# State-space core of a two-layer backbone: where clips, sums and one broadcast are computed

## The chip, the cores and the metric

The kernel runs on one core of a Trainium2 chip. The metric is the device time of one execution in microseconds (us). The kernel before took 1882.75 us in the median of three runs (1881.45 to 1883.67). Its engines are TensorE (PE, matrix products), VectorE (DVE), ScalarE (ACT, table functions and scaled copies), GpSimd (POOL) and SyncE (SP, which issues most transfers). Matrix products read SBUF and write to PSUM banks, which the other engines empty.

## The reference

Two layers work on 256 latent and 256 context tokens of width 1024. Each layer makes one modulated norm and one input projection, feeds three token mixers (a bidirectional state-space scan, a windowed attention, a latent attention), merges them by gates and ends with an FFN. All is fp32. In the last layer the context tokens only feed the mixers and have no output of their own. Cut to what the change touches:

```python
silu_c, silu_cc = silu(c), silu(c_ctx)              # rows of the modulation
mod = silu_c @ w_mod[i] + b_mod[i]                  # and the same with silu_cc
# state-space branch, 16 heads of 64 in 2 groups, chunks of 128 tokens, state of 128
acs  = cumsum(dt * a)                               # per head, along the chunk
y_diag[i] = sum_j (C_i . B_j) exp(acs_i - acs_j) dt_j x_j      # j <= i, in the chunk
state     = sum_j exp(acs_end - acs_j) dt_j B_j x_j            # leaves the chunk
h_next    = h * exp(acs_end) + state
y_off[i]  = exp(acs_i) (C_i . h)
y = y_forward + reverse(y_backward) + d_skip * x    # both directions
out = rms_norm(y * silu(z), norm_g)
```

The context's last state is the latent tokens' first, in each direction.

## The kernel before, in words

Tokens are four tiles of 128: latent 0 and 1, context 2 and 3. In fp32 a large product is made of three products of rounded parts (`hi` and `lo` of the weights by L132 on ScalarE and L134 on VectorE; the products are L146, L147 and L148). Weights come in blocks `raw`; four `raw`, three `hi` and three `lo` blocks turn round. PSUM has four banks named `mm`, two `s` and two `t`.

`ssm_core` works on steps (group, tile, half of four heads): 16 in layer 0, where all four tiles have an output, 8 in layer 1, where only two have. For each step a matrix of decay exponents per head and direction is fetched by a transfer that spreads one row over 128 partitions (`ef` and `eb`, two tiles of 128x512, L873). Then the step runs through five stages, each one step behind the one before:

- `first`: clip both against the token's own sum, per head (four 128x128 pieces: `ef` by ScalarE at L889, `eb` by VectorE at L890), combine them on GpSimd (L891), and scale the product of C and B (`cb`) by dt (L895).
- `second`: the exponential (L901), dt for the other direction (L905), and the product of both (L906).
- `third`: four small products into one `s` bank (L917); after the second half GpSimd multiplies x by d_skip (L920), the states' products go through `t` banks (L925, scaled by L927 into `yo`), and L929 adds the `s` bank to x.
- `fourth`: GpSimd adds both `yo` (L935). `fifth`: the gate with z and its square sum (L941, L943).

Beside the steps run the state chains: `state_x` multiplies x by its weight on GpSimd (L848, `xd`), `state` makes one product into an `s` bank (L856) and either copies it (L140 on VectorE or L142 on ScalarE, `hst`) or adds it to the decayed state before (L861 and L862). There are six chains per group, two per step in both layers: one for each of the four context passes, and one for each of the two latent tiles that hand on to the other.

`weave` lays the core among the work that fills it (z projection, keys and values, gates): it takes parts of the fill by a cost per step (`F_SSM`). The order on each engine is that of the program; an engine does not overtake itself. So an instruction waits also for all that stands in front of it on its engine.

The rows of silu(c) and silu(c_ctx) are loaded as 2x512 pieces in `masks` (L193 to L200), and `mod_rows` spreads each over 128 partitions by a product with a selecting matrix (L245) and a ScalarE copy (L247). `mod_dve` reduces the modulation weights against them on VectorE (L260).

Of the kernel before, what the change touches and what calls it, by code (L numbers as in the profile page):

```python
# [19 lines left out]
P = 128  # L20
# [67 lines left out]
class Kern:  # L88
# [102 lines left out]
    def masks(self):  # L191
        nc, c = self.nc, self.c
        self.crowd = [self.U(name="crow") for _ in range(2)]  # L193
        for j in range(2):
            nc.sync.dma_start(self.crowd[j][0:2, :], self.d["crow"][:, j * 512 : j * 512 + 512])
        for t in self.crowd:
            th = self.U(name="cth")
            nc.scalar.activation(th[0:2, :], t[0:2, :], AF.Tanh, scale=0.5)
            nc.vector.scalar_tensor_tensor(t[0:2, :], th[0:2, :], 1.0, t[0:2, :], ALU.add, ALU.mult)
            nc.vector.tensor_scalar(t[0:2, :], t[0:2, :], 0.5, None, ALU.mult)  # L200
        self.identb = c.tile([P, P], BF16, name="identb")
        nc.vector.tensor_copy(self.identb, self.ident)
        self.maskb = c.tile([P, 2, P], BF16, name="maskb")
        nc.gpsimd.tensor_scalar(self.maskb[:, 0, :], self.tril, -NEG, NEG, ALU.mult, ALU.add)
        nc.gpsimd.tensor_scalar(self.maskb[:, 1, :], self.triu, -NEG, NEG, ALU.mult, ALU.add)
# [30 lines left out]
    def mod_rows(self):  # L236
        nc = self.nc
        self.nmod = 0
        sel = self.c.tile([P, 2, P], F32, name="sel")
        self.crow = []  # L240
        for s in range(2):
            nc.vector.tensor_copy(sel[0:2, s, :], self.ident[0:2, s : s + 1].to_broadcast([2, P]))
            for j in range(2):
                ps = self.PS("s")
                nc.tensor.matmul(ps, sel[0:2, s, :], self.crowd[j][0:2, :], start=True, stop=True)  # L245
                t = self.U(name="crow")
                nc.scalar.activation(t, ps, AF.Copy)  # L247
                self.crow.append(t)

    def mod_dve(self, l, ch):  # L250
        nc = self.nc
        for m in range(8):
# [3 lines left out]
            for s in range(2):  # L256
                o = self.mod[l][:, ch * 8 + m, s : s + 1]
                for j in range(2):
                    junk = self.S([P, 512], "junk", dt=BF16, bufs=1)
                    nc.vector.tensor_tensor_reduce(junk, raw[j], self.crow[2 * s + j], 1.0,  # L260
# [569 lines left out]
    def ssm_core(self, l, tts, fill):  # L830
# [10 lines left out]
        chains = [(g, *c) for g in range(2) for c in ((2, 0, None, 3), (3, 1, None, 2), (3, 0, 3, 0), (2, 1, 2, 1), (0, 0, 0, 1), (1, 1, 1, 0))]  # L841
        hin, xds = {}, {}

        def state_x(i):
            if i < len(chains):
                g, tt, dr, _, _ = chains[i]
                xd = xds[i] = self.U(name="xd")
                nc.gpsimd.tensor_tensor(v8(xd), v8(self.xs[tt, g]), b64(self.wd[:, tt, dr, hs(g)]), ALU.mult)  # L848

        def state(i):  # L850
            if i >= len(chains):
                return
            g, tt, dr, prev, to = chains[i]
            bt = self.btok[tt // 2][:, (tt % 2) * 256 + g * P : (tt % 2) * 256 + g * P + P]
            ps = self.PS("s")
            nc.tensor.matmul(ps, bt, xds.pop(i), start=True, stop=True)  # L856
# [3 lines left out]
            else:  # L860
                nc.vector.tensor_tensor(v8(hn), v8(hin[g, dr, prev]), b64(self.etot[:, tt, dr, hs(g)]), ALU.mult)  # L861
# [15 lines left out]
        def first(i):  # L877
# [8 lines left out]
            for j in range(4):  # L886
                hh = 8 * g + 4 * q + j
                sl = [e[dr][:, j * P : (j + 1) * P] for dr in range(2)]
                nc.scalar.activation(sl[0], sl[0], AF.Relu, scale=-1.0, bias=self.fg[:, tt, 0, hh : hh + 1])  # L889
                nc.vector.tensor_scalar(sl[1], sl[1], self.fg[:, tt, 1, hh : hh + 1], 0.0, ALU.subtract, ALU.min)  # L890
            nc.gpsimd.tensor_tensor(e[0], e[1], e[0], ALU.subtract)  # L891
# [6 lines left out]
        def second(i):  # L898
            g, tt, q = steps[i]
            e, cb = eb[i], tile_[g, tt]  # L900
            nc.scalar.activation(e[0], e[0], AF.Exp)  # L901
# [6 lines left out]
        def third(i):  # L908
# [9 lines left out]
            if q == 1:  # L918
# [10 lines left out]
                nc.vector.tensor_tensor(xs, xs, yds.pop((g, tt)), ALU.add)  # L929
# [17 lines left out]
        si = 0  # L947
        n = len(steps)
        for i in range(2):
            loads(i)  # L950
            state_x(i)
        for i in range(n + 4):
# [3 lines left out]
            state(si)  # L956
            state(si + 1)
            state_x(si + 2)
            state_x(si + 3)
            si += 2  # L960
# [399 lines left out]
    def layer(self, l, x, h, norm):  # L1360
# [19 lines left out]
        drain(fill)  # L1380
        q = [self.swa_q(l, h, g, tts) for g in range(2)]
# [14 lines left out]
        if not last:  # L1396
            self.mod_rows()
# [271 lines left out]
```

## Time and profile before

| | us | share of the span |
|---|---|---|
| profiled execution, its own time | 1882.14 | |
| its span | 1880.0 | |
| TensorE busy | 1812.1 | 96% |
| VectorE busy | 1436.7 | 76% |
| ScalarE busy | 889.5 | 47% |
| GpSimd busy | 351.0 | 19% |

The span begins with the first instruction and ends with the last; some 2 us of the execution lie around it. Times in the rows below are counted from its start. The core of layer 0 lies at about 150 to 310 us, that of layer 1 at about 1287 to 1390 us. Busy shares are means over the program; within the cores TensorE is less busy and VectorE more than over the whole.

### The profile page before, as it was taken

How to read it: one execution, taken by the hardware profiler on the slowest of the kernel's cores; microseconds unless marked ns; L12 is line 12 of the kernel's file. 1: busy time of each engine (PE TensorE's matmuls, PEld its weight loads, DVE VectorE, ACT ScalarE, POOL GpSimd, SP SyncE). 2: the span in 40 equal slices, each digit the busy share in tenths (PEclk: the TensorE clock that was granted, in tenths of full speed). 3: DMA queues.
4: the chain of work that ended last, by engine and by line, in shares of the span. 5: the costliest groups of instructions: out<-in, count | busy, mean ns of one | idle time of the engine just before them, and what ended most of it. 6: DMA issues, size and time to landing. Idle time of an engine off the chain costs nothing. (4 is left out here: it accounts for less than half of the span.)

```text
span 1880.0 us, 28523 instructions
## 1 busy us (share of the span) xinstructions
PE 1812.1 (96%) x10188; PEld 1541.4 (82%) x10188; DVE 1436.7 (76%) x3162; ACT 889.5 (47%) x1931; POOL 351.0 (19%) x297
## 2 busy tenths in 40 slices
PE   8998999999999999999999999998889999999999
PEld 2786777788878888898888888886779988899999
DVE  3888886798799885569988875898878677777654
ACT  3555564444555653343222222546545676555442
POOL 3004434200012331100000000012433245410000
PEclk9999999999999999999999999999899999999999
DMA  8334252355343233535555553435233332255564
GB/s 296 96 107 138 92 177 88 123 194 171 134 153 114 97 118 117 186 117 191 189 203 191 182 160 105 126 100 179 95 128 117 122 105 73 86 182 172 187 177 138
DMA packets 102181, 269.18 MB, mean 143 GB/s; under 512 B 12836, under 2 KB 15700, under 8 KB 102040
## 3 DMA queue, kind: packets, MB, share of 16 engines
q1 hardware_dynamic: 93320, 253.02, 41.3%
q10 hardware_dynamic: 7056, 9.85, 1.5%
q0 software_dynamic: 1664, 4.50, 0.6%
q8 instruction: 80, 1.31, 0.3%
q14 instruction: 61, 0.50, 0.1%
HBM read 255.66 MB, written 11.67 MB: 142 GB/s over the span
## 5 line engine op out<-in xcount | busy, mean ns | idle before, releaser
L132 ACT ACTIVATE hi<-raw 128x1024 fp32r<-128x1024 f32 (+1 forms) x350 | 356.7, 1021 | 586.6 <-PE mm L147 301.8
L134 DVE TENSOR_TENSOR lo<-raw,hi 128x1024 fp32r<-128x1024 f32 (+3 forms) x346 | 420.5, 1217 | 202.9 <-ACT hi L132 201.2
L146 PE MATMUL mm<-hh,hi 128*128 128x512 f32 (+1 forms) x1280 | 439.0, 345 | 3.5 <-ACT sq L683 1.9
L148 PE MATMUL mm<-hh,lo 128*128 128x512 f32 (+1 forms) x1280 | 436.4, 342 | 0.9 <-DVE lo L134 0.9
L147 PE MATMUL mm<-hl,hi 128*128 128x512 f32 (+1 forms) x1280 | 436.6, 342 | 0.6 <-DVE hl L353 0.5
L146 PEld LDWEIGHTS mm<-hh,hi 128*128 128x128 f32 x1280 | 242.1, 190 | 32.3 <-ACT sq L683 2.2
L148 PEld LDWEIGHTS mm<-hh,lo 128*128 128x128 f32 x1280 | 242.8, 190 | 28.7 <-DVE lo L134 1.3
L147 PEld LDWEIGHTS mm<-hl,hi 128*128 128x128 f32 x1280 | 243.0, 190 | 28.3 <-DVE hl L353 1.2
L146 PE MATMUL mm<-hi,hh 128*128 128x512 f32 (+2 forms) x368 | 146.2, 398 | 4.5 <-DVE z L826 2.5
L147 PE MATMUL mm<-lo,hh 128*128 128x512 f32 (+2 forms) x368 | 141.2, 384 | 0.3 <-DVE lo L134 0.3
L148 PE MATMUL mm<-hi,hl 128*128 128x512 f32 (+2 forms) x368 | 137.7, 383 | 2.0 <-DVE hl L353 2.0
L260 DVE CUSTOM_DVE_ANT_0 junk<-mraw,crow,mod 128x512 bf16<-128x512 f32 x160 | 120.3, 752 | 4.8 <-DMA mraw<-in_w_modT 2.3
L260 DVE CUSTOM_DVE_ANT_0 junk<-mraw,crow 128x512 bf16<-128x512 f32 x160 | 110.3, 690 | 9.5 <-DMA mraw<-in_w_modT 7.9
L638 ACT ACTIVATE prob<-s,nm 128x512 f32<-128x512 f32 (+1 forms) x96 | 59.2, 617 | 65.5 <-DVE nm L635 35.1
L146 PEld LDWEIGHTS mm<-hi,hh 128*128 128x128 f32 x368 | 70.7, 192 | 20.1 <-DVE z L826 5.0
L160 POOL TENSOR_TENSOR nrs<-nv,mhalf 128x2 f32<-128x2 f32 x7 | 5.2, 748 | 436.1 <-DVE nv L301 436.1
L153 ACT ACTIVATE pth<-t 128x256 fp32r<-128x256 f32 x160 | 60.7, 387 | 52.0 <-DVE ptl L154 43.3
L147 PEld LDWEIGHTS mm<-lo,hh 128*128 128x128 f32 x368 | 70.6, 192 | 14.1 <-issue 4.1
L148 PEld LDWEIGHTS mm<-hi,hl 128*128 128x128 f32 x368 | 69.6, 191 | 14.8 <-DVE hl L353 2.5
L146 PE MATMUL mm<-acth,hi 128*128 128x512 f32 (+1 forms) x198 | 72.7, 367 | 0.6 <-DVE xl L1346 0.6
L147 PE MATMUL mm<-actl,hi 128*128 128x512 f32 (+1 forms) x198 | 72.3, 365 | 0.0
L148 PE MATMUL mm<-acth,lo 128*128 128x512 f32 (+1 forms) x198 | 72.3, 365 | 0.0
(434 smaller groups left out, 4125.6 us busy)
## 6 DMA issues: line engine op xcount, KB each, us to landing
raw<-in_w_fi SPq DMA_DIRECT2D x88, 512.0 KB, 3.3
mraw<-in_w_modT SPq DMA_DIRECT2D x160, 256.0 KB, 4.6
raw<-in_w_g SPq DMA_DIRECT2D x48, 512.0 KB, 3.3
raw<-in_w_p SPq DMA_DIRECT2D x48, 512.0 KB, 3.3
raw<-in_w_fo SPq DMA_DIRECT2D x32, 512.0 KB, 3.9
raw<-in_w_xbc SPq DMA_DIRECT2D x24, 512.0 KB, 3.5
wm<-in_w_mod SPq DMA_DIRECT2D x32, 256.0 KB, 5.6
raw<-in_w_z SPq DMA_DIRECT2D x16, 512.0 KB, 3.2
```

The source lines that it names most:

```text
L132: nc.scalar.activation(hi[:, :n], raw[:, :n], AF.Copy)
L134: eng.tensor_tensor(lo[:, :n], raw[:, :n], hi[:, :n].bitcast(F32), ALU.subtract)
L146: mm(out, a[0], b[0], start=start, stop=False)
L147: mm(out, a[0], b[1], start=False, stop=False)
L148: mm(out, a[1], b[0], start=False, stop=stop)
L153: nc.scalar.activation(hi, src, AF.Copy)
L160: self.nc.gpsimd.tensor_tensor(out, v, self.mhalf[:, 0 : v.free_size()], ALU.pow)
L260: nc.vector.tensor_tensor_reduce(junk, raw[j], self.crow[2 * s + j], 1.0, o if j else 0.0, ALU.mult, ALU.add, o)
L638: nc.scalar.activation(pt[:, :nk], ps[:, :nk], AF.Exp, bias=nm, scale=scale, accum_out=den)
```

## The change

Four edits, all in or near the core.

1. The rows of silu(c) come by four transfers that spread a row of 512 over 128 partitions, issued behind the fill of the core; tanh and its product are then made on 128x512. The factor one half moves into the reduction. The products and copies of L245 and L247 are gone.
2. In layer 1 the two context tiles make one state sum per direction: the weights `wd` of the farther tile are first multiplied by the nearer one's decay, and two products add up in one bank. Chains per group go from six to four, and a plan says which chains belong to which step.
3. Both clips are ScalarE's (`Relu` with scale -1 gives the negative of what VectorE gave), so GpSimd adds, and the exponential takes the scale -1.
4. The inner product's bank is added to the first `yo` instead of x.

```diff
-        self.crowd = [self.U(name="crow") for _ in range(2)]
-        for j in range(2):
-            nc.sync.dma_start(self.crowd[j][0:2, :], self.d["crow"][:, j * 512 : j * 512 + 512])
-        for t in self.crowd:
-            th = self.U(name="cth")
-            nc.scalar.activation(th[0:2, :], t[0:2, :], AF.Tanh, scale=0.5)
-            nc.vector.scalar_tensor_tensor(t[0:2, :], th[0:2, :], 1.0, t[0:2, :], ALU.add, ALU.mult)
-            nc.vector.tensor_scalar(t[0:2, :], t[0:2, :], 0.5, None, ALU.mult)
...
         self.crow = []
         for s in range(2):
-            nc.vector.tensor_copy(sel[0:2, s, :], self.ident[0:2, s : s + 1].to_broadcast([2, P]))
             for j in range(2):
-                ps = self.PS("s")
-                nc.tensor.matmul(ps, sel[0:2, s, :], self.crowd[j][0:2, :], start=True, stop=True)
                 t = self.U(name="crow")
-                nc.scalar.activation(t, ps, AF.Copy)
+                nc.sync.dma_start(t.rearrange("p (a w) -> p a w", a=1), self.d["crow"][s : s + 1, j * 512 : j * 512 + 512].partition_broadcast(P))
                 self.crow.append(t)
+        yield
+        for t in self.crow:
+            th = self.U(name="crth")
+            nc.scalar.activation(th, t, AF.Tanh, scale=0.5)
+            nc.vector.scalar_tensor_tensor(t, th, 1.0, t, ALU.add, ALU.mult)
...
-                    nc.vector.tensor_tensor_reduce(junk, raw[j], self.crow[2 * s + j], 1.0,
+                    nc.vector.tensor_tensor_reduce(junk, raw[j], self.crow[2 * s + j], 0.5,
...
-        chains = [(g, *c) for g in range(2) for c in ((2, 0, None, 3), (3, 1, None, 2), (3, 0, 3, 0), (2, 1, 2, 1), (0, 0, 0, 1), (1, 1, 1, 0))]
+
+        last = len(tts) == 2
+        if last:
+            steps_ = (((2, 3), 0, None, 0), ((3, 2), 1, None, 1), ((0,), 0, 0, 1), ((1,), 1, 1, 0))
+            for i, (a, b) in enumerate(((2, 3), (3, 2))):
+                nc.vector.tensor_tensor(self.wd[:, a, i, :], self.wd[:, a, i, :], self.etot[:, b, i, :], ALU.mult)
+        else:
+            steps_ = (((2,), 0, None, 3), ((3,), 1, None, 2), ((3,), 0, 3, 0), ((2,), 1, 2, 1), ((0,), 0, 0, 1), ((1,), 1, 1, 0))
+        chains = [(g, *c) for g in range(2) for c in steps_]
         hin, xds = {}, {}
 
         def state_x(i):
             if i < len(chains):
-                g, tt, dr, _, _ = chains[i]
-                xd = xds[i] = self.U(name="xd")
-                nc.gpsimd.tensor_tensor(v8(xd), v8(self.xs[tt, g]), b64(self.wd[:, tt, dr, hs(g)]), ALU.mult)
+                g, tiles, dr, _, _ = chains[i]
+                xds[i] = []
+                for tt in tiles:
+                    xd = self.U(name="xd")
+                    nc.gpsimd.tensor_tensor(v8(xd), v8(self.xs[tt, g]), b64(self.wd[:, tt, dr, hs(g)]), ALU.mult)
+                    xds[i].append(xd)
 
         def state(i):
             if i >= len(chains):
                 return
-            g, tt, dr, prev, to = chains[i]
-            bt = self.btok[tt // 2][:, (tt % 2) * 256 + g * P : (tt % 2) * 256 + g * P + P]
+            g, tiles, dr, prev, to = chains[i]
...
-            nc.tensor.matmul(ps, bt, xds.pop(i), start=True, stop=True)
+            for j, (tt, xd) in enumerate(zip(tiles, xds.pop(i))):
+                bt = self.btok[tt // 2][:, (tt % 2) * 256 + g * P : (tt % 2) * 256 + g * P + P]
+                nc.tensor.matmul(ps, bt, xd, start=j == 0, stop=j == len(tiles) - 1)
             hn = self.U(name="hst")
             if prev is None:
                 self.copy(dr == 0, hn, ps)
             else:
-                nc.vector.tensor_tensor(v8(hn), v8(hin[g, dr, prev]), b64(self.etot[:, tt, dr, hs(g)]), ALU.mult)
+                nc.vector.tensor_tensor(v8(hn), v8(hin[g, dr, prev]), b64(self.etot[:, tiles[0], dr, hs(g)]), ALU.mult)
                 nc.vector.tensor_tensor(hn, hn, ps, ALU.add)
...
-                nc.scalar.activation(sl[0], sl[0], AF.Relu, scale=-1.0, bias=self.fg[:, tt, 0, hh : hh + 1])
-                nc.vector.tensor_scalar(sl[1], sl[1], self.fg[:, tt, 1, hh : hh + 1], 0.0, ALU.subtract, ALU.min)
-            nc.gpsimd.tensor_tensor(e[0], e[1], e[0], ALU.subtract)
+                for dr in range(2):
+                    nc.scalar.activation(sl[dr], sl[dr], AF.Relu, scale=-1.0, bias=self.fg[:, tt, dr, hh : hh + 1])
+            nc.gpsimd.tensor_tensor(e[0], e[1], e[0], ALU.add)
...
-            nc.scalar.activation(e[0], e[0], AF.Exp)
+            nc.scalar.activation(e[0], e[0], AF.Exp, scale=-1.0)
...
-                nc.vector.tensor_tensor(xs, xs, yds.pop((g, tt)), ALU.add)
+                nc.vector.tensor_tensor(yo[0], yo[0], yds.pop((g, tt)), ALU.add)
...
-        si = 0
         n = len(steps)
+        plan = [[0], [1], [2, 3], [4], [5], [6], [7]] if last else [[2 * i, 2 * i + 1] for i in range(6)]
+        plan += [[]] * (n + 5 - len(plan))
...
-            state(si)
-            state(si + 1)
-            state_x(si + 2)
-            state_x(si + 3)
-            si += 2
+            for j in plan[i]:
+                state(j)
+            for j in plan[i + 1]:
+                state_x(j)
...
+        rows = iter(()) if last else self.mod_rows()
+        next(rows, None)
...
-            self.mod_rows()
+            drain(rows)
```

The order of instructions on an engine shows what moves. Names carry buffer numbers, which differ between the two kernels. First VectorE in layer 1, where the first `s` bank of a latent tile is freed (`lo` is the second half of a weight block, `yo` the output from the states). Before:

```order
L890 TENSOR_SCALAR eb_12647<-eb_12647,du_11616 128x128 x4
L890 TENSOR_SCALAR eb_12761<-eb_12761,du_11616 128x128 x4
L890 TENSOR_SCALAR eb_12874<-eb_12874,du_11616 128x128 x3
L134 TENSOR_TENSOR lo_13143<-raw_13140,hi_13142 128x1024
L927 TENSOR_TENSOR yo_12961<-t_12959,du_11617 128x512
L927 TENSOR_TENSOR yo_12965<-t_12963,du_11617 128x512
L929 TENSOR_TENSOR xs_12465<-xs_12465,s_12877 128x512
L140 COPY hst_12970<-s_12968 128x512
```

Now:

```order
L867 TENSOR_TENSOR hst_12872<-hst_12872,s_12870 128x512
L889 TENSOR_TENSOR cb_12887<-t_12885,c_tril 128x128
L910 SCALAR_TENSOR_TENSOR eb_12638<-cb_12887,du_11605,eb_12638 128x128 x4
L911 TENSOR_TENSOR ef_12637<-ef_12637,eb_12638 128x512
L134 TENSOR_TENSOR lo_13116<-raw_13113,hi_13115 128x1024
L932 TENSOR_TENSOR yo_12944<-t_12942,du_11606 128x512
L932 TENSOR_TENSOR yo_12948<-t_12946,du_11606 128x512
L934 TENSOR_TENSOR yo_12944<-yo_12944,s_12860 128x512
L140 COPY hst_12954<-s_12951 128x512
```

The eleven clips in front are gone; the dt products of a step (L910) and its closing product (L911), which stood behind the freed bank, now stand in front of it. The cast and both `yo` stay there, and the sum takes the place of the old one.

Next ScalarE a little later in layer 1, up to the evacuations of keys and values (`kraw`). Before:

```order
L142 ACTIVATE hst_12974<-s_12972 128x512
L889 ACTIVATE ef_13059<-ef_13059,du_11616 128x128 x4
L132 ACTIVATE hi_13178<-raw_13176 128x1024
L901 ACTIVATE ef_12873<-ef_12873 128x512
L901 ACTIVATE ef_12950<-ef_12950 128x512
L901 ACTIVATE ef_13059<-ef_13059 128x512
L132 ACTIVATE hi_13226<-raw_13224 128x1024
L1005 ACTIVATE kraw_13112<-mm_12839 128x256
```

Now:

```order
L132 ACTIVATE hi_13151<-raw_13149 128x1024
L895 ACTIVATE eb_13040<-eb_13040,du_11605 128x128
L895 ACTIVATE ef_13039<-ef_13039,du_11605 128x128
L895 ACTIVATE eb_13040<-eb_13040,du_11605 128x128
L895 ACTIVATE ef_13039<-ef_13039,du_11605 128x128
L895 ACTIVATE eb_13040<-eb_13040,du_11605 128x128
L906 ACTIVATE ef_13039<-ef_13039 128x512
L132 ACTIVATE hi_13199<-raw_13197 128x1024
L142 ACTIVATE hst_13051<-s_13048 128x512
L1011 ACTIVATE kraw_13085<-mm_12822 128x256
```

Clips (L895) stand between the casts and the exponentials (L906), and a copy of a state, `hst`, stands behind the second cast. On VectorE the state additions that stood behind the second half of this cast (L862) have no counterpart there.

Last TensorE in layer 0, at the first place where rows were spread (`crow` is a row, `sel` the selecting matrix). Before:

```order
L1070 MATMUL t_2995<-c_ident,ro_2848 128x128
L1070 MATMUL t_2995<-c_ident,ro_2896 128x128
L1070 MATMUL t_2995<-c_ident,qraw_2782 128x128
L1070 MATMUL t_2995<-c_ident,qraw_2787 128x128
L245 MATMUL s_3078<-crow_1272,sel 128x512
L245 MATMUL s_3082<-crow_1273,sel 128x512
L989 MATMUL t_3027<-c_ident,z_1714 128x128
L989 MATMUL t_3027<-c_ident,z_1717 128x128
```

Now:

```order
L1076 MATMUL t_2991<-c_ident,ro_2844 128x128
L1076 MATMUL t_2991<-c_ident,ro_2892 128x128
L1076 MATMUL t_2991<-c_ident,qraw_2778 128x128
L1076 MATMUL t_2991<-c_ident,qraw_2783 128x128
L146 MATMUL s_3085<-kTh_2223,qTh_2946 128x512
L147 MATMUL s_3085<-kTl_2224,qTh_2946 128x512
L148 MATMUL s_3085<-kTh_2223,qTl_2947 128x512
L1104 LDWEIGHTS identb
L1104 MATMUL s_3085<-maskb,identb 128x128
```

The two products are gone from there, and the first attention scores stand in their place; the other two are gone likewise.

## Rows read from the trace of the kernel before

**Rows 1.** Stretch, length; busy us (instructions) of PE, PEld, DVE, ACT, POOL; PEclk, DMA.
```profile
0.00:1880.00 1880.00, 1812.07 (x10188) 1541.40 (x10188) 1436.72 (x3162) 889.46 (x1931) 350.96 (x297) 0.99 0.44 143
150.00:300.00 150.00, 139.53 (x624) 107.10 (x623) 126.35 (x253) 85.30 (x222) 62.83 (x43) 0.98 0.41 130
1287.00:1392.00 105.00, 92.17 (x471) 70.95 (x469) 90.00 (x163) 54.90 (x138) 43.64 (x32) 0.93 0.37 124
```

**Rows 2.** TensorE's waits in layer 0's core: us in all, times, longest us.
```profile
PE s L856 <- DVE xs L929: 3.0, 1, 3.0
PE mm L146 <- DVE z L826: 2.3, 1, 2.3
PE t L1031 <- DVE yo L927: 1.9, 1, 1.9
```

**Rows 3.** TensorE's waits in layer 1's core, columns as in rows 2.
```profile
PE s L856 <- DVE hst L862: 4.5, 1, 4.5
PE s L856 <- DVE xs L929: 2.9, 1, 2.9
PE t L989 <- DVE z L983: 1.9, 1, 1.9
PE s L917 <- DVE ef L906: 1.5, 2, 1.1
```

**Rows 4.** Stretches behind four waits; PEclk is the granted clock; columns as rows 1.
```profile
183.50:187.50 4.00, 4.00 (x10) 2.47 (x10) 4.00 (x5) 0.60 (x1) 3.92 (x4) 0.58 0.64 181
1315.00:1322.00 7.00, 6.59 (x20) 4.97 (x21) 7.00 (x8) 1.88 (x5) 6.58 (x6) 0.76 0.36 138
1334.60:1341.40 6.80, 5.54 (x9) 2.50 (x9) 5.53 (x15) 5.45 (x28) 0.00 (x0) 0.56 0.22 77
1387.00:1393.00 6.00, 5.53 (x21) 4.40 (x22) 3.61 (x7) 2.14 (x4) 0.00 (x0) 0.72 0.44 165
```

**Rows 5.** TensorE in order of time, first of two places: start, us, instruction, count.
```profile
342.67 1.98 PE L245 MATMUL s<-crow,sel 2*128 2x512 f32 x4
```

**Rows 6.** SyncE in order of time, columns as in rows 5.
```profile
1313.92 0.38 SPq L873 DMA_DIRECT2D ef<-scr  x1
```

**Rows 7.** VectorE in order of time, before the first wait of layer 1.
```profile
1310.74 1.59 DVE L890 TENSOR_SCALAR eb<-eb,du 128x128 f32<-128x128 f32 x2
1312.26 1.21 DVE L134 TENSOR_TENSOR lo<-raw,hi 128x1024 fp32r<-128x1024 f32 x1
1313.39 1.27 DVE L927 TENSOR_TENSOR yo<-t,du 128x512 f32<-128x512 f32 x2
1314.59 0.67 DVE L929 TENSOR_TENSOR xs<-xs,s 128x512 f32<-128x512 f32 x1
```

**Rows 8.** Three engines in order of time, before the second wait of layer 1.
```profile
1328.98 1.88 DVE L890 TENSOR_SCALAR eb<-eb,du 128x128 f32<-128x128 f32 x4
1330.99 1.26 POOL L891 TENSOR_TENSOR ef<-eb,ef 128x512 f32<-128x512 f32 x1 [0.80 <-DVE eb L890]
1332.29 0.63 ACT L901 ACTIVATE ef<-ef 128x512 f32<-128x512 f32 x1 [1.44 <-POOL ef L891]
1332.83 1.04 ACT L132 ACTIVATE hi<-raw 128x1024 fp32r<-128x1024 f32 x1
```

**Rows 9.** Line L890 as a whole; VectorE's and ScalarE's clips in a row.
```profile
L890 DVE TENSOR_SCALAR eb<-eb,du x96: 268/276/1396, 152.1 to 1362.0; 128x128 f32<-128x128 f32 x96
1307.02 5.32 DVE L890 TENSOR_SCALAR eb<-eb,du 128x128 f32<-128x128 f32 x11
164.55 3.03 ACT L889 ACTIVATE ef<-ef,du 128x128 f32<-128x128 f32 x10
```

**Rows 10.** VectorE and GpSimd in order of time, tail of layer 1's core.
```profile
1379.59 0.69 DVE L929 TENSOR_TENSOR xs<-xs,s 128x512 f32<-128x512 f32 x1 [1.12 <-POOL xs L920]
1380.35 3.53 POOL L935 TENSOR_TENSOR xs<-xs,yo 128x512 f32<-128x512 f32 x2 [0.80 <-DVE xs L929]
```

**Rows 11.** VectorE in order of time, before the longest wait of layer 0.
```profile
178.94 1.26 DVE L890 TENSOR_SCALAR eb<-eb,du 128x128 f32<-128x128 f32 x2
```

More of the change, by code (lines that the diff above doesn't have):

```diff
@@ L238, in mod_rows @@
         self.nmod = 0
-        sel = self.c.tile([P, 2, P], F32, name="sel")
         self.crow = []
         for s in range(2):
-            nc.vector.tensor_copy(sel[0:2, s, :], self.ident[0:2, s : s + 1].to_broadcast([2, P]))
             for j in range(2):
-                ps = self.PS("s")
-                nc.tensor.matmul(ps, sel[0:2, s, :], self.crowd[j][0:2, :], start=True, stop=True)
                 t = self.U(name="crow")
-                nc.scalar.activation(t, ps, AF.Copy)
+                nc.sync.dma_start(t.rearrange("p (a w) -> p a w", a=1), self.d["crow"][s : s + 1, j * 512 : j * 512 + 512].partition_broadcast(P))
                 self.crow.append(t)
+        yield
[3 more added lines that the diff above has]
+            nc.vector.scalar_tensor_tensor(t, th, 1.0, t, ALU.add, ALU.mult)
     def mod_dve(self, l, ch):
@@ L945, in ssm_core @@
         need = {(g, dr, to) for g, _, dr, _, to in chains}
-        si = 0
         n = len(steps)
+        plan = [[0], [1], [2, 3], [4], [5], [6], [7]] if last else [[2 * i, 2 * i + 1] for i in range(6)]
+        plan += [[]] * (n + 5 - len(plan))
         for i in range(2):
             loads(i)
-            state_x(i)
+        for j in plan[0]:
+            state_x(j)
         for i in range(n + 4):
@@ L955, in ssm_core @@
                 third(i - 2)
-            state(si)
-            state(si + 1)
-            state_x(si + 2)
-            state_x(si + 3)
-            si += 2
+            for j in plan[i]:
+                state(j)
+            for j in plan[i + 1]:
+                state_x(j)
             if 0 <= i - 3 < n:
```

## The prediction

> **What bounds the kernel now.** I read the busy time by stretch first. TensorE works 1812 of 1880 us, so over the whole program it is the bound, and an engine that gets lighter gains time only where TensorE stands still. That happens in the two state-space cores: in 150 to 300 us TensorE is busy 139.5 of 150 us, in 1287 to 1392 us 92.2 of 105, with VectorE at 126.4 and 90.0, while ScalarE has 64.7 and 50.1 us free in them [rows 1]. The list of TensorE's waits then says who ends them. In layer 0 the three longest are 3.0, 2.3 and 1.9 us [rows 2], in layer 1 4.5, 2.9 and 1.9 us [rows 3], and the name behind each is VectorE. The reader should see there that the waits are few and long, not many and short: a single late VectorE instruction stops the matrix engine.
>
> The third view is the granted clock by stretch. Behind the long waits it falls from 2.4 to 1.2 GHz for a while. What such a stretch costs is its length times the share of the clock that is missing: 4.0 x 0.42 = 1.7 us after the 3.0 us wait of layer 0; 7.0 x 0.24 = 1.7, 6.8 x 0.44 = 3.0 and 6.0 x 0.28 = 1.7 us at the three waits of layer 1 [rows 4]. So a wait that shrinks enough gives back more than itself.
>
> **The change, part by part.** The profiled execution took 1882.14 us, 2.1 us of it around its span of 1880.0, and 0.6 us less than the median of the runs, 1882.75. The sum is made against 1882.14 and 0.6 is added at the end.
>
> Rows of silu(c). The four matrix products that spread them go, in two places. In each place four records stand in 1.98 us [rows 5], back to back with other products, so TensorE loses 2 x 1.98 = 3.96 us of work. No other engine ends in those places. Added are four broadcast transfers, four tanh and four multiplications of 128x512. A broadcast issue holds SyncE 0.38 us, a multiplication of that size costs VectorE 0.64 (two in 1.27), a 128x512 table function on ScalarE 0.63 [rows 6 to 8]: 1.5, 2.5 and 2.5 us, in a stage where TensorE is the bound. The four copies of before go, so ScalarE is even. On the queue of SyncE the four issues stand ahead of weight loads; cover gone, they cost at most those 1.5 us. The trace of before has no such transfer landing; from both sides it is bounded by nothing and by 4 us, the whole gain of this edit, if the rows come late for the reductions that follow. I take nothing, since those reductions run beside matrix work. The eight tiny ScalarE and VectorE operations at the masks go as well, ahead of the core, where neither was waited for: nothing.
>
> Clips. 96 VectorE clips (64 in layer 0, 32 in layer 1) become ScalarE's. Their median is 0.276 us and their longest 1.396; in a crowded stretch eleven took 5.32 us, 0.48 each, while ten on ScalarE took 3.03, so 0.30 each [rows 9]. ScalarE gets 64 x 0.30 = 19 us in layer 0 on top of 85.3 of 150, and 32 x 0.30 = 9.6 us in layer 1 on top of 54.9 of 105: 70% and 62%. It does not become full, but its instructions run in order, and the casts of the weights now stand behind clips. The Trainium skill, "VectorE: DVE Perf Modes" (section "Mode 2×_2P — use both read ports for one tensor"), speaks against this edit: a clip by a scalar on fp32 data in SBUF is the kind of instruction VectorE does two elements at a time, so it moves from the engine that is fastest at it. The rows agree as far as the undisturbed clip goes, 0.276 us, and not in the crowded stretch, where it was dearer than ScalarE's 0.30; by the rule alone VectorE would be relieved of 26 us instead of about 46 at the crowded price, both estimates.
>
> First wait of layer 1 (2.9 us). VectorE's queue in front of it runs without a break: eleven clips of 5.32 us [rows 9], of which the last two take 1.59, a cast of 1.21, two multiplications of 1.27, then the sum that frees the bank [rows 7]. The clips leave this queue. In their place come four products of 128x128 and one of 128x512 of a step that stood behind the bank before; at no more than 0.64 each they are 3.2 us, so at least 2.1 us are won in the queue. But they wait for that step's exponential, and the cast for its first half, which on ScalarE now stand behind clips. So I take only what the last two clips held, 1.59 us; if the exponential is late nothing is won, if all is in time the whole 2.9. The new sum stands where the old one did, and the old one did not wait for GpSimd here, so the earlier release wins nothing by itself. With 1.3 us left of the wait I expect the clock to stay up, since the shortest wait behind which rows 4 show it down is 1.9: 1.59 + 1.68 = 3.3 us.
>
> Second wait (4.5 us). Here a chain is seen link by link: four clips on VectorE, 1.88 us, GpSimd's difference, the exponential, and the weight cast that stood behind that exponential on ScalarE [rows 8]; behind the cast come its second half and the state's addition on VectorE, the one that the wait names [rows 3]. With one state sum for the context chunks that addition is gone: the bank is emptied by a ScalarE copy that stands behind only a cast that is not held by VectorE. The state of the next tile must still wait for GpSimd's multiplication, which stands behind one more addition than before, but the clips that feed it start earlier. I take the wait as gone, with its clock loss: 4.5 + 3.0 = 7.5 us. The eight multiplications and additions that go from VectorE, 5.1 us at 0.64, are otherwise hidden. What is late next is GpSimd's queue; from the other side the edit could win nothing, or lose one addition, 1.3 us.
>
> Tail of layer 1 (1.9 us). The sum waited 1.12 us for GpSimd, and GpSimd's additions waited for the sum. Now the sum runs beside GpSimd's multiplication: what stood between them, 1380.35 - 1379.59 = 0.76 us, goes [rows 10]. The wait falls to 1.1, and with it the clock loss: 0.76 + 1.68 = 2.4 us.
>
> Layer 0. At its 3.0 us wait two clips of 1.26 us stood in the queue [rows 11], so 1.74 is left; the clock loss I count by half, 0.84, as that is close to the 1.9 behind which it fell. Together 2.1 us. The other two I take as unchanged: what ScalarE is given (32 clips before 190 us) stands ahead of the evacuations and casts for which VectorE then waits.
>
> Sum: 3.96 + 3.3 + 7.5 + 2.4 + 2.1 = 19.3 us. 1882.1 - 19.3 + 0.6 = 1863.5 us. Its own range is 1857 to 1869: the halves of the clock terms (3 us) and the three layer-0 or transfer prices taken as nothing.
>
> **The rivals.**
> All waits close. VectorE falls from 84% of layer 0's core to about two thirds, so every named wait may go: 3.0 + 2.3 + 1.9 + 1.7 in layer 0, 4.5 + 2.9 + 1.9 + 6.4 in layer 1, and 4.0: 28.6 us, 1854. For it speaks that all of them end on VectorE; against it that the queue in front of them holds casts and multiplications that stay.
>
> ScalarE's order takes over. A weight cast behind eight clips is up to 2.4 us later than behind four, and what VectorE does next depends on it. Then half of each layer-1 term stays and layer 0 gives nothing: 4.0 + 6.6 = 10.6 us, 1872. For it speaks that in rows 8 a cast behind an exponential was the link that cost most; against it ScalarE's free third.
>
> The waits are replaced one for one, so that the edits of the core move nothing: only the matrix products are won, 1879. That the release does not release, since the sum stays behind the same cast in VectorE's queue, would be part of this.
>
> Slower. Both clips of a step are now in one queue, so GpSimd's addition can start only after eight at 0.30 instead of four: 1.2 us more on every step's chain. If the inner products then wait for their decay factors, once for each of the 12 pairs of group and tile, that is 12 x 1.2 - 4.0 = 10.5 us more, 1893. It decides from the point at which ScalarE has no slack before a step's exponential. Against it: TensorE waited for such factors only 1.5 us in all in layer 1, in two waits [rows 3], and steps are loaded two ahead. By the skill's rule above the clip itself is dearer on ScalarE, which is on this side.
>
> **How the numbers follow.** Forecast 0.55, all waits close 0.13, ScalarE's order 0.18, one for one 0.07, slower 0.07. A measurement of this kernel can tell about 0.2%, 3.8 us, from no change. The first three are faster; one for one lies on that border at 3.9 us and is split, 0.03 and 0.04. Faster 0.89, same 0.04, slower 0.07. A range of 1852 to 1878 leaves out the slower case, most of one for one, and the far end of the best.
>
> **What would show it.** In the new profile the two spread places have no such products; VectorE has 96 clips fewer and layer 1's core four chains fewer; the 4.5 us wait is gone and the 2.9 us wait is near 1.3; the granted clock between 1300 and 1345 us stays at 2.4 GHz; layer 0 keeps its 2 us waits. I am wrong if TensorE's waits in the cores carry ScalarE's or GpSimd's name, if the sum of waits there does not fall by half in layer 1, or if a wait on the broadcast rows appears.

## The result, and the profile after

The changed kernel takes 1858.1 us in the median of four runs (1856.2 to 1861.5), the kernel before 1883.2 us in the same comparison: a ratio of 0.9865, 95% interval 0.9851 to 0.9879, so 25 us less. In a second comparison the ratio was 0.9873 (0.9860 to 0.9887). The forecast was 1863.5 us with a range of 1852 to 1878.

Of the page of the changed kernel, the engines' busy time and the granted clock in 40 slices:

```profile
PE 1798.1 (97%) x10180; PEld 1535.3 (83%) x10180; DVE 1404.2 (76%) x3058; ACT 915.9 (49%) x2025; POOL 351.7 (19%) x297
...
PEclk9999999999999999999999999999999999999999
```

The same two stretches as in [rows 1], the second moved to where layer 1's core now lies; columns as there:

```profile
150.00:300.00 150.00, 145.83 (x672) 114.04 (x671) 114.17 (x200) 104.15 (x280) 63.01 (x45) 1.00 0.42 130
1274.00:1368.00 94.00, 87.54 (x473) 68.46 (x472) 74.75 (x124) 64.46 (x173) 43.27 (x32) 1.00 0.42 137
```

In layer 0 TensorE is busy 145.8 of 150 us where it was 139.5, and the clock is not down at all. ScalarE, busy for 57% of this stretch before, is at 69%, and VectorE is at 76% instead of 84%. None of TensorE's waits listed here ends on ScalarE. TensorE's waits, first from 140 to 320 us, then from 1250 to 1400 us:

```profile
PE t L1037 <- DVE ro L563: 0.9, 1, 0.9
PE s L861 <- DVE yo L934: 0.9, 1, 0.9
PE mm L146 <- DVE z L819: 0.9, 1, 0.9
```

```profile
PE t L790 <- DVE cv L769: 2.7, 1, 2.7
PE t L1076 <- DVE ro L563: 2.4, 1, 2.4
PE t L1076 <- DVE den L609: 1.6, 1, 1.6
PE t L1037 <- DVE yo L932: 1.5, 1, 1.5
PE t L995 <- DVE z L989: 1.4, 1, 1.4
PE s L861 <- DVE hst L867: 0.9, 1, 0.9
```

Against [rows 2] the three waits of layer 0 have shrunk from 3.0, 2.3 and 1.9 to 0.9 us and less; against [rows 3] the two on the state's bank (4.5 and 2.9) are gone and that on z is 1.4; one of 1.5 for `yo` is new. The first row of layer 1 is the convolution ahead of the core, which the change does not touch; it was 2.7 before as well.

Where the time went is read from products that both programs have. Four of them in the kernel before and in the changed one: the convolution ahead of layer 0's core, the first transpose behind it, the convolution ahead of layer 1's core, and the first transpose behind that (start, duration, instruction):

```profile
141.65 0.60 PE L797 MATMUL t<-c_ident,cv 128*128 128x128 f32 x4
317.56 0.60 PE L989 MATMUL t<-c_ident,z 128*128 128x128 f32 x4
1256.48 0.98 PE L797 MATMUL t<-c_ident,cv 128*128 128x128 f32 x7
1387.47 0.30 PE L989 MATMUL t<-c_ident,z 128*128 128x128 f32 x1 [1.92 <-DVE z L983]
```

```profile
140.62 0.60 PE L790 MATMUL t<-c_ident,cv 128*128 128x128 f32 x4
306.71 0.60 PE L995 MATMUL t<-c_ident,z 128*128 128x128 f32 x4
1243.52 0.98 PE L790 MATMUL t<-c_ident,cv 128*128 128x128 f32 x7
1363.86 0.30 PE L995 MATMUL t<-c_ident,z 128*128 128x128 f32 x1 [1.44 <-DVE z L989]
```

| stage | change of the distance to the row above, us | the same in a second execution of the changed kernel | forecast, us |
|---|---|---|---|
| up to the first row | -1.0 | +3.0 | 0 |
| layer 0's core | -9.8 | -9.8 | -2.1 |
| from there to layer 1 (rows of silu(c)) | -2.1 | -0.9 | -4.0 |
| layer 1's convolution and core | -10.7 | -9.7 | -11.5 |
| the rest, to the end of the span | -0.4 | -1.2 | -1.7 |

The sum of the first column is -24.0, the difference of the spans 1880.0 and 1856.0. Of the 13.2 us that were forecast for layer 1, the 1.7 of the clock behind the tail's wait lie behind the last product of the list, so they stand in the last line. What differs at the start is no effect of the change: the two executions of the changed kernel differ there by 4.0 us (last section).

### The profile page after: what moved, and what is told of

It is laid out like the page before. It is cut to its first block, busy times and chain, and to the rows that moved or that the text cites. A ratio compares the mean times of both kernels' runs of the same rounds, so it can differ in the third digit from the quotient of the medians.

```text
span 1856.0 us, 28487 instructions
## 1 busy us (share of the span) xinstructions
PE 1798.1 (97%) x10180; PEld 1535.3 (83%) x10180; DVE 1404.2 (76%) x3058; ACT 915.9 (49%) x2025; POOL 351.7 (19%) x297
```

## The experiments

All ratios are to the kernel before, on the same chip and measured beside it. One us is 0.05%, so ratios whose intervals overlap widely are not told apart. The last two columns are read from one profiled execution of each kernel: by how much the distance between the first two products of the list above differs from that of the kernel before (layer 0's core), and the distance from the third of them to the end of the span (layer 1). Layer 0's column repeats within 0.2 us where nothing of layer 0 was changed. Layer 1's is rougher: the rows alone, which leave that core as it was, are 2.3 us longer there.

| kernel | ratio | 95% interval | won against before, us | layer 0's core, us | layer 1, us |
|---|---|---|---|---|---|
| changed, first and second time | 0.9865, 0.9873 | 0.9851-0.9879, 0.9860-0.9887 | 25, 24 | -9.8, -9.8 | -11.0, -10.9 |
| without the clips | 0.9972 | 0.9962-0.9981 | 5 | -0.1 | -0.8 |
| without the release | 0.9889 | 0.9875-0.9902 | 21 | -9.6 | -9.4 |
| without the state sum | 0.9895 | 0.9881-0.9910 | 20 | -10.0 | -5.2 |
| without the rows | 0.9908 | 0.9894-0.9922 | 17 | -8.2 | -10.8 |
| clips alone | 0.9958 | 0.9944-0.9973 | 8 | -4.0 | -0.9 |
| rows alone | 0.9969 | 0.9956-0.9981 | 6 | -2.8 | +2.3 |
| release and state sum alone | 0.9985 | 0.9976-0.9995 | 3 | +2.6 | -2.4 |
| changed, clips in layer 0 only | 0.9914 | 0.9898-0.9929 | 16 | -9.8 | -2.4 |
| changed, clips in layer 1 only | 0.9923 | 0.9908-0.9939 | 15 | -0.2 | -10.3 |
| changed, rows' products on GpSimd | 0.9917 | 0.9903-0.9931 | 16 | -9.8 | -10.6 |
| changed, rows through a scratch | 0.9859 | 0.9838-0.9881 | 27 | -9.8 | -10.6 |

### One edit undone

**Clips.**

```diff
-                for dr in range(2):
-                    nc.scalar.activation(sl[dr], sl[dr], AF.Relu, scale=-1.0, bias=...fg[:, tt, dr, hh : hh + 1])
-            nc.gpsimd.tensor_tensor(e[0], e[1], e[0], ALU.add)
+                nc.scalar.activation(sl[0], sl[0], AF.Relu, scale=-1.0, bias=...)
+                nc.vector.tensor_scalar(sl[1], sl[1], ..., 0.0, ALU.subtract, ALU.min)
+            nc.gpsimd.tensor_tensor(e[0], e[1], e[0], ALU.subtract)
...
-            nc.scalar.activation(e[0], e[0], AF.Exp, scale=-1.0)
+            nc.scalar.activation(e[0], e[0], AF.Exp)
```

> The changed kernel with the clips of the one direction back on VectorE (GpSimd subtracts, the exponential has no scale). Theory: VectorE's load is what TensorE waited for in layer 0, so most of the 9.8 us won between the two traces in layer 0's core and some 3 us of layer 1's come from the clips; without them about 11 us are lost, near 1869 us, with waits of 2 to 3 us on VectorE and half-clock stretches back in layer 0. Rival: the earlier release of the inner product's bank did it, since its sum no longer waits for GpSimd; then at most 4 us are lost, near 1862.

Measured: 0.9972, so 20 us of the 25 are lost, nearly twice what the theory said. TensorE's waits of this kernel, in layer 0 and then in layer 1:

```profile
PE s L861 <- DVE hst L867: 2.8, 2, 2.7
PE mm L146 <- DVE z L819: 2.6, 1, 2.6
PE t L1037 <- DVE yo L932: 1.9, 1, 1.9
...
PE s L922 <- DVE ef L911: 7.1, 3, 4.7
```

Layer 0 is as in the kernel before: the same three places wait, two stretches at half clock are back, and its core is as long to 0.1 us. In layer 1 the wait for the state's bank is gone, as the state sum has it, but an equal one of 4.7 us stands at the inner products (L922), which wait for their factors. So with the clips in VectorE's queue the other edits only move the wait to the next user of that queue. The rival is refuted.

**Release.**

```diff
-                nc.vector.tensor_tensor(yo[0], yo[0], yds.pop((g, tt)), ALU.add)
+                nc.vector.tensor_tensor(xs, xs, yds.pop((g, tt)), ALU.add)
```

> The changed kernel with the inner product's bank added to x again, behind GpSimd's multiplication by d_skip. Theory: the release stands behind the same cast and products in VectorE's queue either way, so only the tails gain; 1 to 3 us are lost, near 1860. Rival: the release carries layer 0, 8 us or more are lost, 1866 or above, and the wait for that sum before the state's product is back at 3 us in layer 0.

Measured: 0.9889, 3 to 5 us lost by the medians, but the intervals overlap with those of the changed kernel, so the theory's 1 to 3 is not excluded. Layer 0's core is as long as in the changed kernel and its largest wait 1.1 us. The loss that the trace shows is in layer 1's tail, 1.6 us, where TensorE waits for z twice instead of once (1.4):

```profile
PE t L995 <- DVE z L989: 3.4, 2, 2.1
```

Behind the core the clock falls twice, which it does not in the changed kernel. So the rival's mechanism is refuted and the theory's place is right; whether its price is too low is not decided.

**State sum.** The six chains per group and the two chains per step are put back.

```diff
-        if last:
-            steps_ = (((2, 3), 0, None, 0), ((3, 2), 1, None, 1), ((0,), 0, 0, 1), ((1,), 1, 1, 0))
...
+        chains = [(g, *c) for g in range(2) for c in ((2, 0, None, 3), (3, 1, None, 2), (3, 0, 3, 0), (2, 1, 2, 1), (0, 0, 0, 1), (1, 1, 1, 0))]
```

> The changed kernel with six state chains per group in layer 1 again, two per step. Theory: the 4.5 us wait of layer 1 was one for an addition that the single sum has removed, so it comes back in good part with its clock loss; 5 to 7 us are lost, near 1864. Rival: that wait was late because of VectorE's clips and the cast behind the exponential, and is gone with them; at most 2 us are lost, near 1859.

Measured: 0.9895, 4 to 6 us lost, and 5.8 by layer 1's part of the trace. Its longest wait in layer 1 is the old one:

```profile
PE s L849 <- DVE hst L855: 3.8, 1, 3.8
```

The theory holds: the addition that the sum removes is what TensorE waits for, with or without clips in front of it.

**Rows.** The loads in `masks`, the four products and the four copies are put back.

> The changed kernel with the rows of silu(c) spread by matrix products again. Theory: the products cost 4.0 us of TensorE, and the four products of 128x512 that replaced the tiny ones give about 2 us of it back as a wait of the query's rotation behind them on VectorE (the traces differ by 2.1 us in this stage); 2 us are lost, near 1860. Rival: the whole 4 us are the edit's, near 1862, and the 2 us between the traces belong to something else.

Measured: 0.9908, 7 to 8 us lost, more than the rival's 4. In the trace 1.6 us of it are in layer 0's core and 2.6 to 3.8, by which of the two executions of the changed kernel it is set against, between the cores. The order of ScalarE at the start of layer 0's core shows what the theory left out (start, duration, instruction), in this kernel and then in the changed one:

```profile
146.32 1.13 ACT L198 ACTIVATE cth<-crow 2x512 f32<-2x512 f32 x2
151.55 1.06 ACT L132 ACTIVATE hi<-raw 128x1024 fp32r<-128x1024 f32 x1 [4.10 <-PE mm L148]
152.52 0.97 ACT L902 ACTIVATE ef<-ef,du 128x128 f32<-128x128 f32 x3
```

```profile
143.61 0.97 ACT L895 ACTIVATE ef<-ef,du 128x128 f32<-128x128 f32 x3
```

With the two small tanh in the program, a weight cast that waits 4.1 us for TensorE stands ahead of the first clips; without them the clips run in that time. They start 8.9 us earlier, 2.7 us of which are the later start of this one execution (at 140 us it was already that far behind). TensorE then waits 2.7 us for states in layer 0, against 0.4. Five kernels agree in this: with the instructions at the masks (before, without rows, clips alone) this cast stands first, without them (changed, rows alone) the clips do. So two tiny instructions, costed at nothing, go with a worse order; that it is they, and not another part of the same edit, is not shown.

### Edits alone

**Clips** (the first diff, the other way, in the kernel before).

> The kernel before with both clips on ScalarE and nothing else. The three other edits without this one won only 0.28%. Theory: the clips are the main edit and win by themselves, VectorE's queue being what every wait of the cores ended on; 10 to 14 us, ratio near 0.9935, layer 0's waits close to those of the changed kernel, layer 1's 4.5 us wait partly left. Rival: the edits need each other, and clips alone win only what is left when the losses of the three others are taken from the whole, 7 us or less, ratio 0.996 or above.

Measured: 0.9958, 8 us; between the two statements, nearer the rival. Of layer 0's 9.8 us they win 4.0, and a wait for the states is left there; layer 1 wins 0.9, which is within the differences of single traces. The longest wait of layer 0, and then of layer 1:

```profile
PE s L856 <- DVE hst L862: 2.6, 1, 2.6
```

```profile
PE s L856 <- DVE hst L862: 4.7, 1, 4.7
```

In layer 0 the clips need company: with the release (without the rows) they win 8.2 us there, with the rows (without the release) 9.6. In layer 1 the bank of the state's addition is still waited for. Clips alone win next to nothing there, the release and the state sum without clips 0.8 to 2.4 us, clips and release without the state sum 5.2, clips and state sum without the release 9.4. So in layer 1 the clips and the state sum each remove one of two things that were late in the same queue.

**Rows** (in the kernel before).

> The kernel before with the rows of silu(c) by broadcast transfers and nothing else. Theory: what it wins beside 4.0 us of matrix products hangs on ScalarE's order at the start of layer 0's core (with the two small tanh there, the first clips stand behind a weight cast that waits for TensorE); with four clips per step on VectorE, which was the engine waited for, only 1 to 3 us are won, ratio near 0.999. Rival: the edit is worth what its undoing cost in the changed kernel, 8 us, ratio near 0.996.

Measured: 0.9969, 6 us (4 to 8): the theory's 1 to 3 is outside the interval, the rival's 8 at its end, the 4.0 us of products at the other. The theory was wrong to price the order of ScalarE at nothing here: in the trace layer 0's core is 2.8 us shorter, though four clips per step are still VectorE's.

**Release and state sum** (in the kernel before).

> The kernel before with the earlier release and the single state sum of layer 1, clips and rows as they were. Theory: both edits shorten what stands behind VectorE's clips, and as long as the clips are in that queue they win nothing; ratio 0.998 to 1.000 (the three edits without the clips won 0.28%, the rows alone 0.31%). Rival: they are worth what their undoing cost in the changed kernel, 3 to 5 us each, ratio near 0.996.

Measured: 0.9985, 3 us (1 to 5), against the sum of 7 to 10 that undoing the two cost in the changed kernel. The theory holds in that they need the clips gone. But the small sum is made of two parts: layer 1 is 2.4 us shorter, and layer 0's core, where only the release acts, is 2.6 us longer, with a wait that the kernel before has not:

```profile
PE s L929 <- DVE hst L874: 6.2, 1, 6.2
```

Together with the rows (the kernel without the clips) layer 0 is as before.

**The changed kernel again.**

> The changed kernel unaltered, to have its time on the same chip as the next ones: ratio to before near 0.9865. If the losses of the single undone edits are to be read against it, it must lie within 0.1% of that; if it lies nearer 0.989, the losses of 4 to 8 us seen with the release, the states and the rows undone are half as large.

Measured: 0.9873, within 0.1% of 0.9865. The losses above stand, but each is a difference of two ratios with some 2.5 us to either side, so it is uncertain by about 3.5 us: the release's is not told from nothing, the state sum's only just.

### Clips in one layer only

```diff
-                for dr in range(2):
-                    nc.scalar.activation(sl[dr], sl[dr], AF.Relu, ...)
+                nc.scalar.activation(sl[0], sl[0], AF.Relu, ...)
+                if not last:            # the other kernel: if last
+                    nc.scalar.activation(sl[1], sl[1], AF.Relu, ...)
+                else:
+                    nc.vector.tensor_scalar(sl[1], sl[1], ..., 0.0, ALU.subtract, ALU.min)
... (GpSimd's operation and the exponential's scale go with it)
```

> The changed kernel with both clips on ScalarE in layer 0 alone; in layer 1 one of them is VectorE's again. Theory: the clips' 20 us are about 10 in each core, as the ledger of the two traces has it; ratio near 0.992, layer 1's waits of 2 to 5 us on VectorE back. Rival: layer 1's part is the state sum's, so that clips there cost little; ratio 0.988 or below.

> The changed kernel with both clips on ScalarE in layer 1 alone; in layer 0 one of them is VectorE's again. Theory: about 10 us are lost, ratio near 0.992, with the waits of 2 to 3 us and half-clock stretches of layer 0 as in the kernel before. Rival: 15 us or more are lost here, 0.995, since 64 of the 96 clips are layer 0's.

Measured: 0.9914 and 0.9923. Layer 1's clips are worth 8 to 9 us to the changed kernel, layer 0's 9 to 11, and the two losses add up to the 19 to 20 of both. Both theories hold, though layer 0 has twice as many clips. The longest waits of the first kernel in layer 1, and of the second in layer 0:

```profile
PE s L925 <- DVE ef L914: 6.9, 3, 4.5
```

```profile
PE s L861 <- DVE hst L867: 2.8, 2, 2.6
PE mm L146 <- DVE z L819: 2.6, 1, 2.6
PE t L1040 <- DVE yo L935: 1.9, 1, 1.9
```

### The rows' products elsewhere

**On GpSimd.**

```diff
-            nc.vector.scalar_tensor_tensor(t, th, 1.0, t, ALU.add, ALU.mult)
+            nc.gpsimd.tensor_tensor(th, th, t, ALU.mult)
+            nc.gpsimd.tensor_tensor(t, t, th, ALU.add)
```

> The changed kernel, with the product of tanh and row in two GpSimd instructions per row instead of one on VectorE. Theory: the four VectorE products took 3.8 us in a row and held up a rotation that TensorE then waited 1.4 us for; on idle GpSimd they cost nothing, 1 to 2 us are won against the changed kernel, ratio 0.9855. Rival: GpSimd's eight instructions slow VectorE's beside them by as much as clips were slowed beside GpSimd in the core, or the rows come late for the reductions; same or slower than the changed kernel.

Measured: 0.9917, 8 to 10 us worse than the changed kernel. The rival is right, and the trace shows how. TensorE's longest wait at this place, and then VectorE and GpSimd in order of time:

```profile
PE t L1077 <- DVE ro L564: 7.2, 1, 7.2
```

```profile
354.75 0.67 DVE L1328 SCALAR_TENSOR_TENSOR gt<-gt,mm 128x512 f32<-128x512 f32 x1
...
355.94 3.00 POOL L241 TENSOR_TENSOR crth<-crth,crow 128x512 f32<-128x512 f32 x2
...
357.75 1.75 DVE L254 CUSTOM_DVE_ANT_0 junk<-mraw,crow,mod 128x512 bf16<-128x512 f32 x1
358.90 2.97 POOL L242 TENSOR_TENSOR crow<-crow,crth 128x512 f32<-128x512 f32 x2
...
359.42 1.34 DVE L562 TENSOR_TENSOR rt<-qraw,rs 128x128 f32<-128x128 f32 x1
```

The same two instructions in the changed kernel, with GpSimd idle:

```profile
353.53 0.75 DVE L253 CUSTOM_DVE_ANT_0 junk<-mraw,crow,mod 128x512 bf16<-128x512 f32 x1
354.20 0.29 DVE L561 TENSOR_TENSOR rt<-qraw,rs 128x128 f32<-128x128 f32 x1
```

These two instructions are about 1.0 us longer beside GpSimd, whatever their own length: 0.29 becomes 1.34, 0.75 becomes 1.75. Both end only after the GpSimd instruction that was running when they began. The one with an operand in PSUM (`mm`) takes 0.67, with GpSimd busy from 353.7 to 356.0.

**Through a scratch.** Tanh and product on 2x512 ahead of layer 0's convolution, written to memory, and spread from there; nothing is done on 128x512.

> The changed kernel, with silu of the two rows made on 2x512 pieces ahead of layer 0's convolution and written to a scratch in memory, from which the four transfers spread them; no tanh and no product is made on 128x512. Theory: VectorE's 3.8 us and the 1.4 us wait behind them go, 1 to 2 us are won against the changed kernel, ratio near 0.986, and the place behind the core has no wait on the rotation. Rival: the small instructions ahead of the convolution move ScalarE's order as they did at the masks, and cost as much or more; 0.987 or above.

Measured: 0.9859 (0.9838 to 0.9881), not to be told from the changed kernel's. At the place itself the theory holds: the wait for the rotation, in the changed kernel and then here, is

```profile
PE t L1076 <- DVE ro L563: 1.4, 1, 1.4
```

```profile
PE t L1082 <- DVE ro L569: 0.9, 2, 0.6
```

and some 1.5 us are won there between the traces, of which 0.6 are left at layer 1's convolution (against the first execution of the changed kernel). The rival's shift of order did not come: layer 0's core is as long as in the changed kernel. It is the version that I would keep, but that it beats the changed kernel is not shown.

## Why the prediction was right, and where it was not

The direction, the main cause and the range were right: the waits on VectorE in the two cores, with the clock behind them, were what could be won, ScalarE had the room, and no wait on ScalarE or on the broadcast rows appeared. TensorE's waits in layer 1's core (1287 to 1392 us before, 1274 to 1368 now) were 12.9 us in all and are 5.9, so they fell by more than half, as the signs asked. That the sum came out within 6 us owes something to luck: layer 0 was 7.7 us too low, the later stages 4.0 too high (1.9, 0.8 and 1.3).

**Layer 0** is the term that was mis-sized: 2.1 us forecast, 9.8 in both traces. The step that failed is "The other two I take as unchanged": I let ScalarE's order eat what VectorE's lighter queue gave. All three waits of [rows 2] shrank to 0.9 us and less, and TensorE's waits there were 10.4 us in all and are 4.2. The clock is the other part. I counted half of one stretch at half clock; the kernel before has a second one in layer 0, behind the 1.9 us wait (columns as in [rows 4]):

```profile
260.00:267.00 7.00, 5.97 (x21) 4.83 (x22) 7.00 (x13) 2.64 (x9) 3.85 (x3) 0.76 0.30 104
```

Both are gone, 1.7 us each (7.0 x 0.24 here), so waits and clock make 9.6 of the 9.8 us. The kernel with clips in layer 1 only has three waits of 2.6, 2.6 and 1.9 us and both stretches back, and its layer 0 is as long as before: so it takes the clips. It takes the rows or the release as well, since clips alone win 4.0 there. I counted only the clips that stood in the last queue before a wait (1.26 us). But the 64 clips of layer 0 held VectorE for 24.6 us, eleven of them for more than 0.4 each, and its queue was busy for 37 of the 40 us from 150 to 190, so a delay early in it can reach the wait. Whether the clips' own time or their meetings with GpSimd (last section) made the queue late, no run separates.

**Layer 1** was forecast at 13.2, 11.5 and 1.7 by the lines of the table; 10.7 and 0.4 came. Both waits on the state's bank are gone, the first wholly where 1.3 us was to be left, and the clock stays up; against that stands the new wait of 1.5 for `yo`. What the terms did not say is that they are not separate. I gave the 4.5 us wait to the state sum and 1.6 us of the first to the clips; but each alone is worth little in layer 1, and the two together 9.4 of its 11 us. Behind the core the wait for the rotation is 2.4 us and was 1.1, which takes back most of the tail's clock. It is 2.4 in the kernel with the rows alone too, whose core of layer 1 is as before, so it does not come from the edits of the core; what makes it longer is open.

**Rows**: 4.0 us forecast, 2.1 and 0.9 in the two traces, 6 alone and 7 to 8 when undone. The products' 3.96 us of TensorE are certain from [rows 5]. Two things that I took lightly cost time. The four products of 128x512 took 3.8 us on VectorE, not 2.5: GpSimd's scaling of the queries ran beside the first of them until 347.9 us, and two transposes behind them were held up. TensorE's waits from 330 to 400 us, and then the first three of the four products and GpSimd beside them, in the changed kernel:

```profile
PE t L596 <- DVE ptl L154: 1.8, 1, 1.8
PE t L1076 <- DVE ro L563: 1.4, 1, 1.4
```

```profile
342.47 5.47 POOL L1066 TENSOR_TENSOR qraw<-qraw,rsq 128x512 f32<-128x512 f32 x4
345.90 3.18 DVE L241 SCALAR_TENSOR_TENSOR crow<-crth,crow 128x512 f32<-128x512 f32 x3
```

With the rows alone both waits are there, in the kernel before and without the rows neither. And with the tiny instructions at the masks, which I said nobody waits for, ScalarE's order at the start of the core is another one. The case that the rows come late did not arise: the transfers were issued at 282 to 284 us, landed within 5.6 us, and were first read at 344.

**Release**: "wins nothing by itself" at the 2.9 us wait is right, since layer 0 does not change without it; what the trace shows of its loss, 1.6 us, is in the tail, where 2.4 were forecast.

**The rivals.** "All waits close" gave 1854, and layer 0 went that way. The slower case did not come: the wait for decay factors is 0.5 us in layer 0. That the clip is dearer on ScalarE is true by [rows 9] for an undisturbed one (0.276 against 0.30 us) and decided nothing; VectorE was relieved of 38.2 us, between the two estimates of 26 and 46.

Three figures of the prediction are off without weight. ScalarE's share in layer 1 is 61%, not 62. A cast behind eight clips instead of four is 1.2 us later, not 2.4. And the trace of before does have a landing to set the rows against: the transfers of `ef`, which spread a row too, landed in 3.7 to 7.1 us.

## What to carry to other kernels

A wait can be worth more than the instructions in the queue right before it: where an engine's queue has been full for some time, count what is removed from the whole full stretch as what can be won, and add what the clock gives back behind every wait, after listing all stretches at half clock and not only the longest. Edits that relieve the same queue are to be tried together, since each alone may only hand the wait to the next instruction: alone they won 8, 6 and 3 us here, together 25. And an instruction moved to GpSimd to spare VectorE costs VectorE up to one GpSimd instruction each time the two meet on SBUF operands.

## What the runs showed of the hardware

**VectorE and GpSimd exclude each other, for whole instructions.** Two lines of the kernel before that differ only in where the second operand lies, the decay's product in SBUF and the addition from the PSUM bank (shortest, median and longest in ns):

```profile
L861 DVE TENSOR_TENSOR hst<-hst,du x16: 677/684/1776, 153.9 to 1358.0; 128x512 f32<-128x512 f32 x16
...
L862 DVE TENSOR_TENSOR hst<-hst,s x16: 671/676/689, 161.0 to 1358.8; 128x512 f32<-128x512 f32 x16
```

Seven of the sixteen with both inputs in SBUF are 0.16 to 1.1 us longer, and each of the seven began while a GpSimd instruction was running; the other line is never longer, though GpSimd ran beside four of its sixteen. The clip, with one tensor in SBUF, goes from 0.276 to 1.396 us [rows 9]. So the extra is what is left of the GpSimd instruction, up to a whole one (the shortest of 128x512 take 1.04 us), and not a share of one. One decay's product began just before a GpSimd instruction: it and the next took 0.69 us, and the GpSimd instruction beside them 2.2. The Trainium skill, "SBUF — State Buffer" (section "Who interferes with whom"), says that a VectorE instruction with two SBUF inputs, or in a mode that uses both ports, and a GpSimd instruction that reads SBUF shut each other out until the first has ended. The trace agrees with these 16 instructions, and the reductions and rotations above with their 1.0 us.

**The clock is not a function of the kernel alone.** The changed kernel was profiled twice. Both executions have the same TensorE waits of 6.0, 2.0, 1.9 and 1.2 us in the first 110 us. The same two stretches of the first and of the second execution, columns as in [rows 1]:

```profile
0.00:45.00 45.00, 37.16 (x117) 11.95 (x118) 14.90 (x33) 13.77 (x24) 15.05 (x29) 1.00 0.87 309
...
60.00:75.00 15.00, 14.50 (x64) 12.03 (x65) 9.85 (x20) 8.77 (x31) 1.64 (x1) 1.00 0.23 75
```

```profile
0.00:45.00 45.00, 37.40 (x105) 11.43 (x106) 12.56 (x30) 13.25 (x23) 15.30 (x29) 0.97 0.87 304
...
60.00:75.00 15.00, 13.12 (x53) 10.61 (x52) 7.99 (x21) 7.12 (x28) 1.64 (x1) 0.89 0.31 99
```

In the first the granted clock is full in both, in the second it is at 1.2 GHz for part of each, and that execution was 2.4 us behind at 45 us and 4.0 us at 140. The two were profiled at different times and perhaps on different chips, which may have a part in it; but the mean granted clock also differs between the four runs of one comparison, 0.996 to 1.000. So a term of 1.7 us for the clock behind a wait of 2 us is a chance, not a price, and single profiles of one kernel differ by 4 us before the change begins.
